# A two-layer hybrid decoder trunk: the adds that empty PSUM banks get a higher scheduling priority

## The chip, the cores and the metric

The kernel runs on one core of one Trainium2 chip. The metric is the device time of one execution in microseconds (us), and less is better. The median of three runs of the kernel before is 2667.34 us (2663.45 to 2671.42). The five engines of the core appear under their short names: PE is TensorE's matmul, PEld its weight load, DVE is VectorE, ACT is ScalarE, POOL is GpSimd and SP is SyncE, which issues nearly all loads.

## What is computed

The input is one sequence of 256 tokens of width 2048, in fp32. Two layers follow one another, each with a mixer and a feed-forward network (FFN); a final RMSNorm ends them.

```
for layer in (0, 1):
    x = x + mixer[layer](rms_norm(x, g_mix[layer]))      # 0: mLSTM heads and Mamba-2 heads; 1: attention
    x = x + swiglu(rms_norm(x, g_ffn[layer]), w_gate, w_up, w_down)
out = rms_norm(x, g_final)

def swiglu(x, w_gate, w_up, w_down):                     # w_gate, w_up: 2048 x 5632, w_down: 5632 x 2048
    return (silu(x @ w_gate) * (x @ w_up)) @ w_down
```

Only the two FFNs matter here. All weights come from HBM once.

## The kernel before

**Matmuls in three passes.** Each fp32 operand is split into a high part (rounded to the matmul's fp32r type) and a low part (what the rounding left). A product is three matmuls into the same bank: high times high, high times low, low times high (L383, L384, L385). The high part of a weight tile, `wh`, is a ScalarE copy (L355); its low part, `wl`, is a VectorE subtraction (L357).

**A step.** The FFN works in steps of 256 rows of the contraction dimension and 2 x 512 columns (for gate and up: 512 of each; for down: 1024 columns next to one another) by 256 tokens. A plain step (P) is four output tiles of 128 x 512 with two row blocks each, 8 products, 24 matmuls. A seven-product step (S) does the same 2 x 2 block product with seven products, 21 matmuls, in the manner of Strassen and Winograd. For that VectorE forms four sums of weight quarters (L364, L365, L367), so that an S step needs two weight tiles, the raw one and the sums, each with high and low parts. Below, "step 1, raw" and "step 1, sums" are these two.

**Strips and blocks.** `block` (L371) runs the steps of one strip. For gate and up the plan is P S P S P S P P, numbered 0 to 7; 11 strips cover the 5632 hidden columns, in groups of 4, 4 and 3. After each group `down` multiplies its hidden columns with w_down, in two blocks q of 1024 columns each (plan P S P S P P P P, or P S P S P P for the group of 3).

**PSUM.** There are eight banks of 128 x 512. Banks 0 to 3, `acc_f`, hold the four output tiles F of a block from its first to its last step. Banks 4 to 7, `acc_e`, hold the products E that S steps share between tiles. After the last S step (step 5 of a strip) the E banks are joined in four SBUF tiles `pre`: one ScalarE copy and four VectorE adds (L414 to L418). The two plain steps left go on into the F banks. At the end of a gate and up strip, `hidden` adds each F bank to its `pre` (L839), takes tanh on ScalarE (L842) and finishes the hidden values h on VectorE (L843, L844); then eight transposes on TensorE (L223) go into banks of the E ring, are split by L165 and L166, and make the operand of `down`. At the end of a down block, `add_all` adds `pre` and then F into the residual `xres` (L855): the pre part is called from inside `block` right after the last S step, the F part after the block has ended (L862). The next block's step 0 needs the four F banks again.

**Buffers.** A raw weight tile is loaded by two SP loads of 512 KB (L348). There are four buffers for raw tiles and sums, and three each for `wh` and `wl`, used in turn, so that the parts of a tile can be formed only when TensorE is done with the tile three places earlier.

**What sets the order.** All loops are unrolled and a list scheduler writes the order of each engine's instructions at build time: of those that it finds ready, it takes the one with the lowest priority number, which is the place in the program. A block under `tc.high_priority(offset=n)` is given numbers n lower. On the chip each engine runs its instructions in the order so written, with waits between engines. Weight work (`weights`, L340, its sums, copies and subtractions) stands under

```
        with tc.high_priority(offset=800):
            if not summed:
                return parts(raw, (slice(0, 2), slice(2, 4)))
```

while L414 to L418, L839 and L855 have no offset, and neither have L842 to L844 and the transposes.

Of the kernel before, what the change touches and what calls it, by code (L numbers as in the profile page):

```python
# [59 lines left out]
def hybrid_trunk(ctx: ExitStack, tc: tile.TileContext, a: dict, out: bass.AP):  # L60
    nc = tc.nc
# [38 lines left out]
    def blk(shape, name, dt=F32):  # L100
        return held_tile("blk", shape, name, dt)
# [7 lines left out]
    def t2(shape, name, dt=F32):  # L109
        return tmp.tile(shape, dt, tag="tmp", name=name)  # L110
# [7 lines left out]
    def bank(i, name):  # L118
        return psm.tile([P, 512], F32, tag=f"b{i}", name=name)
# [67 lines left out]
    def tick():  # L187
        clock[0] += 1
        run_until(lambda p: held[0] or p[0] > clock[0])
# [6 lines left out]
    class KT:  # L196
# [5 lines left out]
        def block(self, b):  # L202
            if self.blocks[b] is None:
                self.blocks[b] = self.home([P, 4, 2, T], f"{self.name}{b}", F32R)
            return self.blocks[b]
# [54 lines left out]
    def transpose_later(kt, b, src, gcol, wait, step=1):  # L260
        for half in range(2):
            later(wait + half * step, (kt.name, b), transpose_split, kt, b, src, gcol, half)
# [107 lines left out]
    def block(src, kt, row, nk, plan, after_sums=None, lead=1):  # L370

        n = nk // 2
        plan = plan[:n]
        F = [None] * 4
        pre = None
        E = {}

        def add(dst, a, b, start, stop):
            (ah, al), (bh, bl) = a, b
            nc.tensor.matmul(dst, ah, bh, start=start, stop=False)  # L383
            nc.tensor.matmul(dst, ah, bl, start=False, stop=False)  # L384
            nc.tensor.matmul(dst, al, bh, start=False, stop=stop)  # L385

        first_s, last_s = plan.find("S"), plan.rfind("S")
        turn["aux"] = 0
        group = []
        for j in range(n):  # L390
            if plan[j] == "S":
                held[0] = True
                wh, wl, sh, sl = weights(src, row + 2 * j * P, True)
                tok = lambda k, t: tuple(x[:, t * P:(t + 1) * P] for x in kt.parts(k))
                k2, k1 = 2 * j, 2 * j + 1
                a11, a12, a22 = tok(k1, 0), tok(k2, 0), tok(k2, 1)
                sk = kt.sums[j]
                s1, s2, s3, s4 = [(sk[:, i, 0, :], sk[:, i, 1, :]) for i in range(4)]
                b21, b11, b22 = [(wh[:, i, :], wl[:, i, :]) for i in range(3)]
                t3, t1, t2_, t4 = [(sh[:, i, :], sl[:, i, :]) for i in range(4)]  # L400
                prod = {1: (a11, b11), 2: (a12, b21), 3: (s4, b22), 4: (a22, t4),
                        5: (s1, t1), 6: (s2, t2_), 7: (s3, t3)}
                for p in (2, 3, 1, 7, 5, 6, 4):
                    if p in (2, 3, 4):
                        i = p - 2
                        add(F[i], *prod[p], start=False, stop=False)
                    else:
                        if p not in E:
                            E[p] = bank({1: 4, 7: 5, 5: 6, 6: 7}[p], "acc_e")
                        add(E[p], *prod[p], start=j == first_s, stop=j == last_s)  # L410
                if j == last_s:
                    pre = [t2([P, STRIP], "pre") for _ in range(4)]
                    p1, v, u3, w = pre
                    nc.scalar.copy(p1, E[1])  # L414
                    nc.vector.tensor_add(v, p1, E[6])
                    nc.vector.tensor_add(u3, v, E[7])
                    nc.vector.tensor_add(v, v, E[5])
                    nc.vector.tensor_add(w, u3, E[5])  # L418
                    if after_sums is not None:
                        after_sums(pre)  # L420
            else:
                group.append((j, weights(src, row + 2 * j * P, False)))
                if len(group) < lead and j < n - 1 and n - j <= lead:
                    continue
                for i in range(4):
                    t, s = divmod(i, 2)
                    first = F[i] is None
                    if first:
                        F[i] = bank(i, "acc_f")
                    for jj, (wh, wl) in group:  # L430
                        for kk in range(2):
                            xh, xl = kt.parts(2 * jj + kk)
                            ts = slice(t * P, (t + 1) * P)
                            add(F[i], (xh[:, ts], xl[:, ts]), (wh[:, 2 * s + kk, :], wl[:, 2 * s + kk, :]),
                                start=first and jj == group[0][0] and kk == 0, stop=jj == n - 1 and kk == 1)
                group = []
            tick()
            if j == last_s:
                held[0] = False
        return F, pre  # L440
# [168 lines left out]
    v = [blk([P, MH, MDV + 8], f"v{t}")[:, :, :MDV + 1] for t in range(NT)]  # L609
# [215 lines left out]
    def ffn(xt, r, wg_, wu_, wd, name, finish, begin=None):  # L825

        rh = cst.tile([P, NT], F32, tag="rh", name="rh" + name)
        rr = cst.tile([P, NT], F32, tag="rr", name="rr" + name)
        nc.vector.tensor_scalar(rh, r, 0.5, None, op0=OP.mult)
        nc.vector.tensor_mul(rr, rh, r)  # L830

        def hidden(hT, i, s, plan):
            F, pre = block(((wg_, s * STRIP), (wu_, s * STRIP)), xt, 0, KD, plan)
            hs = []
            for t in range(NT):
                g, u = F[2 * t], F[2 * t + 1]
                if pre is not None:
                    for p, f in zip(pre[2 * t:2 * t + 2], (g, u)):
                        nc.vector.tensor_add(p, p, f)  # L839
                    g, u = pre[2 * t:2 * t + 2]  # L840
                h = t2([P, STRIP], "h")
                nc.scalar.activation(h, g, AF.Tanh, scale=rh[:, t:t + 1])  # L842
                nc.vector.scalar_tensor_tensor(h, h, 1.0, g, op0=OP.add, op1=OP.mult)  # L843
                nc.vector.scalar_tensor_tensor(h, u, rr[:, t:t + 1], h, op0=OP.mult, op1=OP.mult)  # L844
                hs.append(h)
            transpose_later(hT, i, hs, None, 1, 0)

        def down(hT, first, n, last):
            for q in range(2):
                c0 = 2 * q * STRIP  # L850
                dst = [xr_[t][:, c0 + n_ * STRIP:c0 + (n_ + 1) * STRIP] for t in range(NT) for n_ in range(2)]

                def add_all(what):
                    for d, x in zip(dst, what):
                        nc.vector.tensor_add(d, d, x)  # L855

                if last and begin is not None:
                    begin(2 * q)
                    begin(2 * q + 1)
                F, _ = block(((wd, c0), (wd, c0 + STRIP)), hT, first * STRIP, 4 * n, PLAN_H[n], add_all,  # L860
                             lead=2 if last and q and name == "b" else 1)
                add_all(F)  # L862
                if last:
                    for s in (2 * q, 2 * q + 1):
                        finish(s)

        ring["aux"] = (6, 7, 4, 5)
        first = 0
        for n in (4, 4, 3):
            hT = KT(f"h{name}{first}", 4 * n)  # L870
            hT.sums = {j: None for j in range(2 * n) if PLAN_H[n][j] == "S"}
            for i in range(n):
                hidden(hT, i, first + i, PLAN_X)
            down(hT, first, n, first + n == DFF // STRIP)
            first += n
        ring["aux"] = (6, 7)
        turn["acc"] = 4
# [155 lines left out]
```

## Time and profile before

| | |
|---|---|
| median of 3 runs | 2667.34 us |
| profiled execution, its time | 2665.1 us |
| its span, first to last instruction | 2663.0 us |
| mean granted TensorE clock | 0.994 |
| PE busy | 2596.1 us (97%) |
| PEld busy | 2146.9 us (81%) |
| DVE busy | 2036.7 us (76%) |
| ACT busy | 1416.9 us (53%) |
| read from HBM | 492.39 MB, 186 GB/s over the span |

The profile is one execution, recorded by the hardware profiler. In the span, 0 to 780 us are the mixer of layer 0 and its output projection, 780 to 1530 the first FFN, 1530 to 1930 the attention layer, 1930 to the end the second FFN and the last norm. Rows of grouped instructions read: line, engine, operation, written tile <- read tiles, shape, count, then busy time and mean duration in ns, then the engine's idle time just before them and what ended it. Rows of waits read: engine, tile and line that waited <- what it waited for: total us, number of times, longest. Rows of stretches read: from:to, length, busy us (and instructions) of PE, PEld, DVE, ACT and POOL, granted clock, busy share of the DMA engines, GB/s. Rows of a timeline read: start, duration, instruction, how many are merged, and in brackets the idle time before it with what ended it. Matmuls are pipelined: a 128 x 512 matmul has a duration of about 0.39 us in the profile, and one starts every 0.227 us.

### The profile page before, as it was taken

What the parts mean: (1) busy time and instruction counts of PE and PEld (TensorE: products, weight loads), DVE (VectorE), ACT (ScalarE), POOL (GpSimd) and SP (SyncE); (2) the same over time, 40 slices, a digit from 0 to 9 for tenths busy, and PEclk for the clock granted to TensorE, in tenths of its full rate; (3) what the DMA queues carried; (4) which work ended last, traced back from release to release, by engine and by line L of the source; (5) the groups of instructions that cost most, each with busy time, mean ns of one, the idle gap of its engine ahead of it and who ended that gap; (6) DMA issues with size and microseconds to landing.
All of it is one profiled execution on the core that took longest, in us unless ns stands there. A gap on an engine that the chain in (4) does not pass through costs nothing.

```text
span 2663.0 us, 32578 instructions
## 1 busy us (share of the span) xinstructions
PE 2596.1 (97%) x12255; PEld 2146.9 (81%) x12255; DVE 2036.7 (76%) x2568; ACT 1416.9 (53%) x1886; POOL 46.8 (2%) x97
## 2 busy tenths in 40 slices
PE   8999999999999999999999999999999999999997
PEld 7888888888887778778887788888877787778876
DVE  5675777755558988898789766666698878987897
ACT  5455665665445554555454555556554545454554
POOL 2000010000000000000000000000000000000000
PEclk9999999999999999999999999999999999999999
DMA  7566676566645555656565465556465655565654
GB/s 231 167 191 182 184 228 190 166 189 216 189 156 189 191 198 188 203 186 203 176 206 173 143 191 173 173 173 205 142 215 175 206 175 204 175 206 175 207 171 150
DMA packets 254765, 496.66 MB, mean 187 GB/s; under 512 B 15704, under 2 KB 16096, under 8 KB 254352
## 3 DMA queue, kind: packets, MB, share of 16 engines
q1 hardware_dynamic: 250816, 484.57, 56.5%
q0 software_dynamic: 2896, 8.51, 1.2%
q8 instruction: 96, 1.57, 0.2%
q10 hardware_dynamic: 896, 1.52, 0.2%
q14 instruction: 61, 0.50, 0.1%
HBM read 492.39 MB, written 2.14 MB: 186 GB/s over the span
## 4 chain that ended last, share of the span: by engine, by line
PE 71%; DVE 16%; DMA 7%; issue 4%; ACT 2%; SPq 0%; POOL 0%; DVEq 0%; ACTq 0%; POOLq 0%
PE acc_w L304 11%; DVE wl L357 9%; PE acc_f L383 8%; PE acc_f L384 8%; PE acc_f L385 8%; PE acc_a L334 8%; PE acc_a L336 8%; PE acc_a L335 8%; PE acc_w L306 5%; DMA raw<-in_l_ffn_up 4%; DMA raw<-in_l_ffn_down 2%; ACT wh L355 2%; DVE sums L364 1%; PE p_tr L223 1%; PE acc_e L383 1%
## 5 line engine op out<-in xcount | busy, mean ns | idle before, releaser
L290 DVE TENSOR_TENSOR wl<-raw,wh 128x1024 fp32r<-128x1024 f32 (+1 forms) x385 | 469.8, 1221 | 324.7 <-ACT wh L289 323.1
L355 ACT CAST wh<-raw 128x1024 fp32r<-128x1024 f32 (+1 forms) x438 | 477.9, 1139 | 373.6 <-PE acc_f L385 295.3
L357 DVE TENSOR_TENSOR wl<-raw,wh 128x1024 fp32r<-128x1024 f32 (+1 forms) x438 | 563.6, 1329 | 119.7 <-ACT wh L355 119.7
L289 ACT CAST wh<-raw 128x1024 fp32r<-128x1024 f32 (+1 forms) x385 | 403.1, 1047 | 391.1 <-PE acc_a L336 181.4
L383 PE MATMUL acc_f<-wh,x 128*128 128x512 f32 x1012 | 397.2, 394 | 25.0 <-DVE pre L839 23.9
L384 PE MATMUL acc_f<-wl,x 128*128 128x512 f32 x1012 | 397.9, 393 | 1.3 <-DVE wl L357 1.2
L385 PE MATMUL acc_f<-wh,x 128*128 128x512 f32 x1012 | 395.9, 391 | 0.0
L355 ACT CAST wh<-sums 128x1024 fp32r<-128x1024 f32 x180 | 182.2, 1051 | 227.5 <-PE acc_f L385 89.1
L304 PE MATMUL acc_w<-xa,wh 128*128 128x512 f32 x768 | 275.9, 403 | 1.1 <-DVE xa L169 1.1
L383 PEld LDWEIGHTS acc_f<-wh,x 128*128 128x128 f32 x1012 | 190.9, 189 | 72.6 <-DVE pre L839 31.1
L357 DVE TENSOR_TENSOR wl<-sums,wh 128x1024 fp32r<-128x1024 f32 x180 | 213.4, 1220 | 23.1 <-ACT wh L355 23.1
L384 PEld LDWEIGHTS acc_f<-wl,x 128*128 128x128 f32 x1012 | 191.2, 189 | 47.8 <-DVE wl L357 8.4
L385 PEld LDWEIGHTS acc_f<-wh,x 128*128 128x128 f32 x1012 | 191.1, 189 | 39.5
L306 PE MATMUL acc_w<-xa,wl 128*128 128x256 f32 x768 | 215.5, 282 | 0.0
L304 PE MATMUL acc_w<-x,wh 128*128 128x512 f32 x512 | 185.0, 405 | 0.0
L304 PEld LDWEIGHTS acc_w<-xa,wh 128*128 128x128 f32 x768 | 144.9, 189 | 34.2 <-ACT wh L289 1.5
L334 PE MATMUL acc_a<-wh,xa 128*128 128x512 f32 x384 | 151.4, 394 | 0.0
L336 PE MATMUL acc_a<-wh,xa 128*128 128x512 f32 x384 | 151.2, 394 | 0.0
L335 PE MATMUL acc_a<-wl,xa 128*128 128x512 f32 x384 | 150.2, 391 | 0.0
L306 PEld LDWEIGHTS acc_w<-xa,wl 128*128 128x128 f32 x768 | 145.6, 190 | 0.8
L306 PE MATMUL acc_w<-x,wl 128*128 128x256 f32 x512 | 143.4, 281 | 0.0
L364 DVE TENSOR_TENSOR sums<-raw 128x1024 f32<-128x1024 f32 x90 | 109.9, 1221 | 27.2 <-DMA raw<-in_l_ffn_up 20.7
(320 smaller groups left out, 4612.2 us busy)
## 6 DMA issues: line engine op xcount, KB each, us to landing
raw<-in_l_w_in SPq DMA_DIRECT2D x191, 512.0 KB, 3.6
raw<-in_l_ffn_gate SPq DMA_DIRECT2D x176, 512.0 KB, 3.9
raw<-in_l_ffn_up SPq DMA_DIRECT2D x176, 512.0 KB, 4.8
raw<-in_l_ffn_down SPq DMA_DIRECT2D x176, 512.0 KB, 5.2
raw<-in_l_w_qkv SPq DMA_DIRECT2D x96, 512.0 KB, 3.6
raw<-in_l_w_out SPq DMA_DIRECT2D x64, 512.0 KB, 4.6
raw<-in_l_w_o SPq DMA_DIRECT2D x32, 512.0 KB, 4.7
rows<-scr POOLq DMA_DIRECT2D x10, 512.0 KB, 6.1
```

Of the source, the lines that this page charges most:

```text
L289: nc.scalar.copy(wh[:, ks, :], raw[:, ks, :])
L290: nc.vector.tensor_sub(wl[:, ks, :], raw[:, ks, :], wh[:, ks, :].bitcast(F32))
L304: nc.tensor.matmul(banks[f], wh[:, kk, fs], kt.both(k), start=k == 0, stop=False, skip_group_check=True)
L306: nc.tensor.matmul(banks[f][:, :T], wl[:, kk, fs], kt.parts(k)[0], start=False, stop=k == nk - 1, skip_group_check=True)
L334: nc.tensor.matmul(banks[t], xh[:, ts], wh[:, kk, :], start=k == 0, stop=False)
L335: nc.tensor.matmul(banks[t], xh[:, ts], wl[:, kk, :], start=False, stop=False)
L336: nc.tensor.matmul(banks[t], xl[:, ts], wh[:, kk, :], start=False, stop=k == nk - 1)
L355: nc.scalar.copy(h[:, c, :], of[:, c, :])
L357: nc.vector.tensor_sub(l[:, c, :], of[:, c, :], h[:, c, :].bitcast(F32))
L383: nc.tensor.matmul(dst, ah, bh, start=start, stop=False)
L384: nc.tensor.matmul(dst, ah, bl, start=False, stop=False)
L385: nc.tensor.matmul(dst, al, bh, start=False, stop=stop)
```

## The change

Three places get `tc.high_priority(offset=1600)`: the join of the E banks, the four adds of the F banks at the end of a gate and up strip, and the last call of `add_all`, which adds the F banks of a down block into the residual. Their offset is then larger than the 800 of the weight work. The additions of `pre` to the residual inside a down block, the tanh, L843, L844 and the transposes keep their place. No instruction is added or taken away.

```diff
@@ block, after the last S step
                     p1, v, u3, w = pre
-                    nc.scalar.copy(p1, E[1])
-                    nc.vector.tensor_add(v, p1, E[6])
-                    nc.vector.tensor_add(u3, v, E[7])
-                    nc.vector.tensor_add(v, v, E[5])
-                    nc.vector.tensor_add(w, u3, E[5])
+                    with tc.high_priority(offset=1600):
+                        nc.scalar.copy(p1, E[1])
+                        nc.vector.tensor_add(v, p1, E[6])
+                        nc.vector.tensor_add(u3, v, E[7])
+                        nc.vector.tensor_add(v, v, E[5])
+                        nc.vector.tensor_add(w, u3, E[5])
                     if after_sums is not None:
                         after_sums(pre)
@@ hidden
                     for p, f in zip(pre[2 * t:2 * t + 2], (g, u)):
-                        nc.vector.tensor_add(p, p, f)
+                        with tc.high_priority(offset=1600):
+                            nc.vector.tensor_add(p, p, f)
@@ down
-                add_all(F)
+                with tc.high_priority(offset=1600):
+                    add_all(F)
```

## The prediction

> **What bounds the kernel now.** I read the page first, then busy time by stage, then what TensorE waited for, then one strip boundary in the timeline of TensorE and VectorE.
>
> ```profile
> span 2663.0 us, 32578 instructions
> PE 2596.1 (97%) x12255; PEld 2146.9 (81%) x12255; DVE 2036.7 (76%) x2568; ACT 1416.9 (53%) x1886; POOL 46.8 (2%) x97
> ```
>
> ```profile
> 780.00:1530.00 750.00, 725.96 (x3194) 587.80 (x3192) 644.43 (x727) 383.97 (x420) 1.38 (x2) 0.99 0.55 185
> 1930.00:2663.00 733.00, 700.00 (x3069) 566.55 (x3068) 631.43 (x710) 369.10 (x396) 1.10 (x2) 0.99 0.56 187
> 888.34:932.75 44.41, 43.02 (x192) 34.91 (x192) 40.71 (x48) 24.38 (x26) 0.00 (x0) 1.00 0.57 190
> ```
>
> TensorE (first busy column) bounds the span. The two FFN stages (780 to 1530 and 1930 to 2663) hold 24.0 + 33.0 = 57 us of its 66.9 us of idle time; only they contain the changed lines, so the change can give at most about that, plus what a slow clock costs. One strip of 512 gate and up columns (third row) takes 44.4 us, TensorE busy 43.0, VectorE (third busy column) 40.7: VectorE is close behind.
>
> ```profile
> PE acc_f L383 <- DVE pre L839: 29.5, 21, 1.9
> PE acc_f L383 <- DVE xres L855: 5.1, 4, 2.4
> PE acc_e L384 <- DVE wl L357: 4.1, 6, 1.5
> ```
>
> Half of TensorE's idle time is one wait: the first matmul into an F bank, for the add (L839) that empties the bank of the strip before, 21 times, 1.4 us each. Low parts of weights (wl) cost it only 4.1 us. One boundary, TensorE first, then VectorE:
>
> ```profile
> 927.80 0.39 PE L383 MATMUL acc_f<-wh,x 128*128 128x512 f32 x1
> 930.97 0.39 PE L385 MATMUL acc_e<-wh,skx 128*128 128x512 f32 x1
> 932.75 0.50 PE L383 MATMUL acc_f<-wh,x 128*128 128x512 f32 x1 [1.39 <-DVE pre L839]
> 936.97 1.03 PE L223 MATMUL p_tr<-ident,h 128*128 128x128 f32 x8
> 937.76 0.48 PE L383 MATMUL acc_f<-wh,skx 128*128 128x512 f32 x1
> ```
>
> ```profile
> 913.49 4.63 DVE L357 TENSOR_TENSOR wl<-raw,wh 128x1024 fp32r<-128x1024 f32 x4 [1.22 <-ACT wh L355]
> 918.13 1.23 DVE L364 TENSOR_TENSOR sums<-raw 128x1024 f32<-128x1024 f32 x1
> ...
> 923.34 0.68 DVE L416 TENSOR_TENSOR pre<-pre,acc_e 128x512 f32<-128x512 f32 x1
> 923.94 0.68 DVE L839 TENSOR_TENSOR pre<-pre,acc_f 128x512 f32<-128x512 f32 x1
> 924.54 1.75 DVE L357 TENSOR_TENSOR wl<-raw,wh 128x1536 fp32r<-128x1536 f32 x1
> 926.21 0.68 DVE L417 TENSOR_TENSOR pre<-pre,acc_e 128x512 f32<-128x512 f32 x1
> 926.80 1.21 DVE L364 TENSOR_TENSOR sums<-raw 128x1024 f32<-128x1024 f32 x1
> 927.94 0.68 DVE L418 TENSOR_TENSOR pre<-pre,acc_e 128x512 f32<-128x512 f32 x1
> 928.54 0.68 DVE L365 TENSOR_TENSOR sums<-raw,sums 128x512 f32<-128x512 f32 x1
> 929.14 2.35 DVE L357 TENSOR_TENSOR wl<-sums,wh 128x1024 fp32r<-128x1024 f32 x2
> 931.41 0.68 DVE L367 TENSOR_TENSOR sums<-raw,sums 128x512 f32<-128x512 f32 x1
> 932.01 0.68 DVE L839 TENSOR_TENSOR pre<-pre,acc_f 128x512 f32<-128x512 f32 x1
> ...
> 934.47 0.68 DVE L839 TENSOR_TENSOR pre<-pre,acc_f 128x512 f32<-128x512 f32 x1
> ...
> 935.79 0.75 DVE L844 SCALAR_TENSOR_TENSOR h<-pre,rra,h 128x512 f32<-128x512 f32 x1
> ```
>
> The next strip's first matmul starts at 927.80. Between the first L839 (923.94) and the second (932.01) VectorE does 8 us of the next strip's weights; TensorE has 15 matmuls that need no other bank, then stands until 932.75.
>
> A stall also costs afterwards. The last column but two is the granted clock:
>
> ```profile
> 840.00:845.00 5.00, 5.00 (x13) 3.92 (x14) 4.75 (x8) 1.22 (x2) 0.00 (x0) 0.54 0.54 201
> 1493.00:1497.00 4.00, 3.72 (x10) 2.96 (x11) 2.02 (x4) 2.67 (x8) 0.00 (x0) 0.56 0.28 105
> 1966.00:1971.00 5.00, 4.82 (x15) 3.79 (x16) 3.95 (x8) 1.67 (x2) 0.00 (x0) 0.66 0.53 196
> 2233.00:2238.00 5.00, 4.88 (x14) 3.90 (x15) 3.88 (x7) 0.73 (x1) 0.00 (x0) 0.66 0.60 207
> ```
>
> ```profile
> 837.46 0.59 PE L384 MATMUL acc_e<-wl,skx 128*128 128x512 f32 x1 [1.52 <-DVE wl L357]
> 839.79 0.79 PE L383 MATMUL acc_f<-wh,x 128*128 128x512 f32 x1 [1.32 <-DVE pre L839]
> ```
>
> Two stalls within 2.4 us are followed by five microseconds at 0.54: 5 x 0.46 = 2.3 us lost. The other three stretches lose 4 x 0.44 = 1.8, 5 x 0.34 = 1.7 and 1.7; they follow the longest boundary stalls. 7.5 us in all, 1.8 of it (1493) behind the wait for xres.
>
> The Trainium skill, "TensorE: Matmul & The Clock Gate", section "What's actually happening", says that the clock halves only after an idle window of about 3.4 us. By that rule none of these stalls, each under 2.5 us, would slow the clock, and the clock term below would be nothing; the measured 0.54 decides against it.
>
> **The change part by part.** No instruction is added or removed; three groups are put ahead of weight work in VectorE's order (and the ACT copy L414 in ScalarE's). The order in which the two built programs' instructions stand shows it: until the end of the first strip both are the same; after that the adds of the E banks (L415 to L418) stand between the low parts of the strip's last two weight tiles, and the four L839 between the next strip's first sums, instead of behind the weights for its steps 1 and 3. TensorE's order follows: 24 matmuls of the next strip's step 0 in a row, in place of 6, 9 of step 1, 18.
>
> (1) *F banks.* I walk VectorE through the new order from 913.49. Pitches from the rows above: a 128x1024 low part 4.64 / 4 = 1.16, a 128x512 add 0.60 (923.34 to 923.94), a 128x1536 part 1.67, the large sum 1.14. Up to the first L839 stand six low parts, one 128x512 part of activations, four E adds and one sum: 7.0 + 0.6 + 2.4 + 1.1 = 11.1, so it starts at 924.6 and the second ends at 925.9. TensorE wants the second bank at 927.80 + 6 matmuls x 0.227 = 929.2. The third and fourth add, behind a small sum and the 128x1536 part, end at 928.8 and 929.4; wanted at 930.5 and 931.9. All four are early by 1.7 us or more, so the whole wait goes: 29.5 us. The bounds are 0 (all of it moves, below) and 29.5.
>
> (2) *Clock.* Without these stalls the three slow stretches behind them go: 2.3 + 1.7 + 1.7 = 5.7 us. Bounds 0 and 7.5.
>
> (3) *xres (L855, raised in its last call only).* An F add writes the slice that the unraised add of pre writes before it, and must follow it. In the new order these four still stand up to 14 instructions apart in the last column half. I count no gain: 0 of 5.1 + 1.8 us.
>
> (4) *What is late instead.* The work passed over: the last low parts of step 1, then the multiplies that finish h (L843, L844), then h's transposes. Continued at the same pitches: small sum 929.9, two low parts with one L843 between them 932.9, the sum for step 3 934.0, first L844 934.7, step 2's two low parts 937.0, step 3's sum, part and sum 939.9, L843 and L844 941.2. Before, the last L844 ended at 936.5 and all eight transposes went at 936.97. TensorE, unstalled: step 0 to 933.2, 15 matmuls of step 1 and two transposes to 936.8, 20 matmuls of step 2 to 941.3. There it needs the second h: just there. Low parts of step 2 (935.8, 937.0) are wanted at 936.8 and 938.4. Then come the transposes' banks, which are the E banks:
>
> ```profile
> L165 ACT CAST ha<-p_tr x5: 573/587/592, 896.1 to 986.4; 128x512 fp32r<-128x512 f32 x5
> L166 DVE TENSOR_TENSOR ha<-p_tr,ha x5: 680/684/692, 897.9 to 987.1; 128x512 fp32r<-128x512 f32 x5
> L364 DVE TENSOR_TENSOR sums<-raw 128x1024 f32<-128x1024 f32 x90 | 109.9, 1221 | 27.2 <-DMA raw<-in_l_ffn_up 20.7 <-DMA raw<-in_l_ffn_down 4.2 <-PE acc_a L336 0.7
> L855 DVE TENSOR_TENSOR xres<-xres,acc_f 128x512 f32<-128x512 f32 x48 | 32.2, 682 | 18.4 <-PE acc_f L385 18.4
> ```
>
> The six transposes end near 941.9, two ScalarE copies (0.59 each) at 943.2, while TensorE has four matmuls until 942.8: it waits 0.4 us; the VectorE part that frees the other bank can stand behind a sum waiting for its load (L364: 20.7 us there in the whole run). Each step used later passes this on, since there are only three buffers for high and low parts. I take 0.7 us a boundary, 22 boundaries (11 strips in each of two layers): 15 us. Bounds: 0, where TensorE finds other matmuls, and 1.5 + 2.3 = 3.8 a boundary, the 837.46 event with its slow clock; 0.7 is nearer to 0, because the walk gives 0.4 and low parts cost TensorE 4.1 us in all now.
>
> SP's queue: loads keep their order but for three places, where two loads of one weight tile change places with two of the next. The trace's loads take about 5 us and are wanted over 10 us later: nothing, unless VectorE frees the buffers late, which is part of (4).
>
> The Trainium skill, "PSUM — Partial Sum Buffer", section "Engine vs sequencer instructions", calls VectorE's queue strictly first in, first out: a raised add that is not ready holds the weights behind it. The trace agrees, L855 kept VectorE idle for 18.4 us in 48 adds. By my walk the raised adds are 0.6 us or more behind their banks, so this adds nothing; at 0.4 us for each of 88 adds VectorE would lose 34 us, and that case is inside the third rival.
>
> Sum: 29.5 + 5.7 + 0 - 15 = 20.2 us. The profiled execution took 2665.1 us with 2663.0 of span; 2665.1 - 20 = 2645. The runs' median, 2667.3, is 2.2 higher; I forecast 2646.
>
> **The rivals.** (a) *All of it is gained.* TensorE's order has other matmuls at each place in (4), and the xres waits shrink too: 29.5 + 7.5 + 5.1 = 42, 2625. For it: in the clean half of the strips the order takes nothing apart. Against: VectorE's 40.7 of 44.4 us leaves little to catch up with. (b) *The wait only moves*, to E banks or low parts, one for one: 35.2 / 22 = 1.6 us a boundary, 2667. (c) *Slower: low parts come late.* Place: the second half of step 3's weights, whose buffers come free only when the E matmuls held up by the late transposes are done. In 12 strips of the new order these matmuls stand taken apart and mixed with step 4's; in 2 of the old one, and one of these two led to the 837.46 event. At 3.8 us in the 16 strips that follow a strip: 61 - 35 = 26, 2693; in the ten new ones alone, 38 + 5 for the rest - 35 = 8, 2675. It decides from 1.6 us a boundary. For it, the missing cover in (4); against, that event needed VectorE to be behind at a boundary as well, which the raised adds prevent for the banks. (d) *No slow clock to regain* (the skill's rule above): without the 5.7 the sum is 14.5, 2651 to 2653; the rows speak against it, chance 0.05, counted within the forecast.
>
> **How the numbers follow.** Forecast (2634 to 2659) 0.46, (a) 0.20, (b) 0.13, (c) 0.21. A difference under 0.3% (8 us) is about what a measurement of this kernel can't tell from none, so (b) is "same". Faster is 0.66, same 0.13, slower 0.21. The range goes from 2622 (under which some 0.08 of (a) lies) to 2684 (some 0.1 of (c) above).
>
> **What would show it.** TensorE's wait for L839 under 5 us; wait for ACT's p_tr copies, wl or wh of some 10 to 20 us in its place; no granted clock under 0.7 within the FFN strips; strip period near 43.5 us; ScalarE's wait of h on L839 mostly gone. The forecast is wrong if TensorE's waits for wl pass 30 us, if 0.5 clocks come more often, or if L839 itself waits for TensorE for more than a few us.

## The result and the profile after

The changed kernel takes 2609.12 us (median of four runs, 2607.17 to 2611.76); beside it the kernel before took 2669.38 us. The ratio is 0.9778 [0.9757, 0.9798]: 60 us faster, where 20 were forecast, and below the range given. The profiled execution took 2609.47 us, that of before 2665.1, so the two traces are 55.6 us apart. From the page of the profile after, the span and the engines:

```profile
span 2607.7 us, 32610 instructions
PE 2579.4 (99%) x12255; PEld 2142.8 (82%) x12255; DVE 2039.9 (78%) x2568; ACT 1417.5 (54%) x1886; POOL 46.9 (2%) x97
```

The two FFN stages of the kernel after, as stretches:

```profile
780.00:1505.00 725.00, 718.74 (x3206) 587.22 (x3205) 648.09 (x729) 385.70 (x423) 1.38 (x2) 1.00 0.57 192
1880.00:2602.00 722.00, 715.79 (x3180) 584.64 (x3178) 647.72 (x728) 380.43 (x410) 1.80 (x3) 1.00 0.57 189
```

TensorE's waits of the kernel after, the largest that belong to the FFNs:

```profile
PE acc_f L383 <- DVE xres L857: 1.7, 1, 1.7
PE acc_f L383 <- ACT wh L355: 1.1, 2, 0.9
...
PE acc_e L383 <- ACT wh L355: 1.0, 2, 0.5
PE acc_f L384 <- DVE wl L357: 1.0, 2, 0.6
```

The wait for the adds that empty the F banks (L839 before, L841 here) is gone from the list, and nothing of size has taken its place: TensorE has 6.3 + 6.2 = 12.5 us of idle time in the two stages, where it had 57.0. From the first FFN matmul's start to the last one's, the stages take 709.1 and 705.3 us where they took 736.1 and 735.0; the time between them is the same (391.1 before, 391.8 after). So all of the gain, 27.0 + 29.7 = 56.7 us, lies in the FFNs.

To see where it came from I put down, for every two TensorE instructions that follow one another in the FFN stages of the timeline, the distance of their starts beyond the usual 0.227 us for a matmul and 0.098 us for a transpose. It belongs to the releaser that the later one, or a weight load between them, shows; the distance right after a stall, some 0.11 us longer than usual, is counted with the stall, and any other matmul pitch of 0.33 to 0.48 us without a releaser is put down as slow clock. The same was done for each experiment below (us, both FFNs together). The last column is from the order of TensorE's instructions as built: in how many of the 34 strips and down blocks the 24 matmuls of step 0 stand in a row.

| kernel | FFN stages | F adds | high and low parts (wh, wl) | xres | late h, ha, hb, xg | slow clock | step 0 whole |
|---|---|---|---|---|---|---|---|
| before | 1471.1 | 36.0 | 20.6 | 6.9 | 0.5 | 5.7 | 5 |
| after | 1414.4 | 0 | 7.0 | 1.9 | 5.3 | 0 | 32 |
| F adds alone | 1442.0 | 13.5 | 13.9 | 7.4 | 3.5 | 3.2 | 10 |
| join (E adds) alone | 1479.9 | 6.8 | 58.6 | 2.1 | 5.9 | 8.6 | 3 |
| last down add alone | 1459.6 | 35.9 | 18.1 | 2.0 | 0.8 | 2.4 | 12 |
| F and down | 1434.3 | 13.6 | 13.4 | 1.9 | 3.6 | 1.8 | 17 |
| join and down | 1472.4 | 6.5 | 53.8 | 0.6 | 6.2 | 7.3 | 10 |
| h alone | 1498.0 | 49.0 | 19.9 | 7.2 | 0.6 | 20.2 | 5 |
| after, rank 800 | 1416.4 | 0 | 7.6 | 2.2 | 4.8 | 1.3 | 32 |
| after, h raised | 1408.3 | 0 | 7.6 | 2.0 | 0.4 | 0 | 32 |
| after, h and xres raised | 1404.8 | 0 | 6.3 | 0 | 0.4 | 0 | 34 |
| before, weights unranked | 1405.1 | 0 | 6.6 | 0.8 | 0 | 0 | 33 |

From before to after: F adds 36.0, clock 5.7, xres 5.0, and 13.6 from fewer waits for the parts of weights, which no term of the prediction had; against it stand 4.8 of new waits for what is now late. That is 55.5 of the 56.7 us, and small unnamed gaps are the rest.

The boundary that the prediction walked through, in the kernel after: VectorE's timeline first, then rows of TensorE's matmuls and weight loads.

```profile
914.24 0.68 DVE L419 TENSOR_TENSOR pre<-pre,acc_e 128x512 f32<-128x512 f32 x1
914.84 1.22 DVE L357 TENSOR_TENSOR wl<-raw,wh 128x1024 fp32r<-128x1024 f32 x1
915.98 1.22 DVE L364 TENSOR_TENSOR sums<-raw 128x1024 f32<-128x1024 f32 x1
917.11 1.28 DVE L841 TENSOR_TENSOR pre<-pre,acc_f 128x512 f32<-128x512 f32 x2
918.31 0.68 DVE L365 TENSOR_TENSOR sums<-raw,sums 128x512 f32<-128x512 f32 x1
918.91 1.75 DVE L357 TENSOR_TENSOR wl<-raw,wh 128x1536 fp32r<-128x1536 f32 x1
920.58 1.27 DVE L841 TENSOR_TENSOR pre<-pre,acc_f 128x512 f32<-128x512 f32 x2
...
931.64 0.75 DVE L846 SCALAR_TENSOR_TENSOR h<-pre,rra,h 128x512 f32<-128x512 f32 x1
932.30 0.68 DVE L845 SCALAR_TENSOR_TENSOR h<-h,pre 128x512 f32<-128x512 f32 x1
933.02 0.75 DVE L846 SCALAR_TENSOR_TENSOR h<-pre,rra,h 128x512 f32<-128x512 f32 x1
```

```profile
932.44 0.44 PE L223 MATMUL p_tr<-ident,h 128*128 128x128 f32 x2
933.87 0.83 PE L223 MATMUL p_tr<-ident,h 128*128 128x128 f32 x6
```

```profile
933.83 0.64 PEld L223 LDWEIGHTS p_tr<-ident,h 128*128 128x128 f32 x6 [0.22 <-DVE h L846]
936.47 0.19 PEld L383 LDWEIGHTS acc_e<-wh,skx 128*128 128x128 f32 x1 [0.37 <-DVE ha L166]
```

The four F adds stand within 4.7 us (917.11 to 921.85), where they took 11.2 (923.94 to 935.15, the prediction's rows). The price stands in the rows behind: h is ready 16.7 us after the first add, the transposes go in two portions at the end, and TensorE waits 0.2 to 0.4 us for h and ha.

### The profile page after: what moved, and what is told of

Its sections match the earlier page's. It is cut to its first block, busy times and chain, and to the rows that moved or that the text cites. A ratio compares the mean times of both kernels' runs of the same rounds, so it can differ in the third digit from the quotient of the medians.

```text
span 2607.7 us, 32610 instructions
## 1 busy us (share of the span) xinstructions
PE 2579.4 (99%) x12255; PEld 2142.8 (82%) x12255; DVE 2039.9 (78%) x2568; ACT 1417.5 (54%) x1886; POOL 46.9 (2%) x97
## 4 chain that ended last, share of the span: by engine, by line
PE 94%; DVE 3%; DMA 1%; issue 1%; ACT 1%; SPq 0%; POOL 0%; ACTq 0%; POOLq 0%; DVEq 0%
PE acc_f L384 14%; PE acc_f L385 14%; PE acc_f L383 14%; PE acc_w L304 11%; PE acc_a L334 8%; PE acc_a L336 8%; PE acc_a L335 8%; PE acc_w L306 6%; PE acc_e L383 3%; PE acc_e L384 3%; PE acc_e L385 3%; PE p_tr L223 2%; DVE wl L357 1%; PE p_y L763 1%; DMA raw<-in_l_ffn_up 0%
```

## The experiments

Two ideas were tried against one another first. **A**: the three raised groups work independently, each on its own wait. **B**: they are one chain. An F add writes the tile that the join writes before it, so a raised add is held by a join that was not raised.

**F adds alone.**

```diff
                     for p, f in zip(pre[2 * t:2 * t + 2], (g, u)):
-                        nc.vector.tensor_add(p, p, f)
+                        with tc.high_priority(offset=1600):
+                            nc.vector.tensor_add(p, p, f)
```

> Only the four adds of the F banks in hidden (L839) get the offset of 1600; the join of the E banks and the last add_all of a down block keep their place. Theory A (the F adds alone were late, each part works by itself): nearly all of the 60 us comes back, 40 to 52 us faster than before, some 2620; TensorE's wait for L839 is under 4 us. Theory B (an F add writes the tile that the join writes first, so a join left behind the weights holds the raised adds): 15 to 35 us faster, some 2645, and waits for L839 stay at 10 to 20 us.

Measured: 2637.62 us (2636.55 to 2639.8), ratio 0.9879 [0.9864, 0.9894], 33 us faster. The waits of TensorE in this kernel:

```profile
PE acc_f L383 <- DVE pre L840: 9.7, 13, 1.5
PE acc_f L383 <- DVE xres L856: 6.2, 3, 2.9
```

Over half of the gain comes from this one line, but a third of the F bank wait is still there, though the adds have the rank that they have in the changed kernel. Idea B had 15 to 35 us, and 10 to 20 us of this wait.

**The join alone.**

```diff
-                    nc.scalar.copy(p1, E[1])
-                    nc.vector.tensor_add(v, p1, E[6])
...
+                    with tc.high_priority(offset=1600):
+                        nc.scalar.copy(p1, E[1])
+                        nc.vector.tensor_add(v, p1, E[6])
...
```

> Only the join of the E banks is raised. Theory A: no gain (within 5 us of before), since the next strip needs the E banks late and the L839 adds stay behind the weights. Theory B: also little by itself, 0 to 10 us faster, from F adds that can follow the join sooner; TensorE's wait for L839 stays above 20 us in both. Were it above 25 us faster, it is the join and not the F adds that held the boundary.

Measured: 2673.91 us (2670.08 to 2677.52), ratio 1.0016 [1.0007, 1.0026]: no gain, if anything 4 us lost. Its waits of TensorE:

```profile
PE acc_e L383 <- ACT wh L355: 14.2, 21, 0.9
PE acc_e L384 <- DVE wl L357: 12.4, 11, 1.6
PE acc_f L383 <- ACT wh L355: 8.2, 26, 0.9
...
PE acc_f L383 <- DVE pre L840: 1.2, 4, 0.5
```

Here the wait did only move. The F bank wait falls by 29 us in the table, and the waits for parts of weights rise by 38. Both ideas had missed this: they left the wait for the F adds above 20 us, and its row reads 1.2. The built order shows with what it goes together: in 22 of the 34 blocks step 0 is taken apart behind its twelfth matmul, with parts of step 1 and of step 2 or 3 between its pieces, so that the weight tiles of several steps are in use at once; there are three buffers for parts.

**The last down add alone.**

```diff
-                add_all(F)
+                with tc.high_priority(offset=1600):
+                    add_all(F)
```

> Only the last add_all of a down block is raised. Both theories: the waits for xres shrink from 6.9 us to 2 to 5 us by the spacing of the matmuls, the waits for L839 stay at 30 us or more, 2 to 7 us faster than before.

Measured: 2660.46 us (2653.22 to 2661.51), ratio 0.996 [0.9946, 0.9973], 10 us faster, more than the 2 to 7 expected. TensorE's wait at the strips stays as it was:

```profile
PE acc_f L383 <- DVE pre L839: 29.9, 21, 1.9
```

The xres waits fall from 6.9 to 2.0 us, and over half of the slow clock goes with them (5.7 to 2.4).

**F adds and the last down add**, both edits from above.

> F adds and the last add_all of a down block raised, the join not. Theory A: 50 to 60 us faster, the whole change but for some 5 us. Theory B: 20 to 40 us faster; the join is worth 20 us or more on top of the F adds though it is worth little alone.

Measured: 2628.34 us (2624.83 to 2629.64), ratio 0.9841 [0.9826, 0.9856], 42 us faster, about the 33 + 10 of the two alone: these add up. TensorE's wait for the F adds is that of the F adds alone:

```profile
PE acc_f L383 <- DVE pre L840: 9.6, 15, 1.5
```

What the changed kernel has beyond this one is the raised join: 0.9841 - 0.9778 = 0.0063 of 2670 us, 17 us (each of the two ratios is known to 0.002 or better, some 5 us). Alone it was worth nothing. In the table the waits for the F adds go from 13.6 to 0 with it and those for parts from 13.4 to 7.0. That speaks for B, though B had put this kernel at 20 to 40 us and the join at 20 or more.

**The join and the last down add**, the missing combination.

> The changed kernel without its raised F adds: the join of the E banks and the last add of the down projections are raised. Together with the five kernels of before, F, E and down alone, F with down, and all three, it fills the table of parts. Theory B (the join is worth its 18 us only because the raised F adds stand behind it): without raised F adds the join adds nothing to the down part, 2655 to 2666 us. Theory A (the parts add up: the join is worth 18 us beside the down part): 2640 to 2648 us.

Measured: 2666.06 us (2662.04 to 2671.27), ratio 0.9976 [0.9966, 0.9987], at the upper end of what B expected (2666) and far from A. Its waits of TensorE are much like those of the join alone:

```profile
PE acc_e L383 <- ACT wh L355: 12.5, 17, 0.9
PE acc_e L384 <- DVE wl L357: 10.7, 9, 1.3
```

So the join is worth +4 us alone (0.0016 of 2670), +4 us beside the down add (0.9976 - 0.996), and -17 us beside the F adds. B is supported, A is out.

**The raised groups at the rank of the weights**: 800 in place of 1600 at all three places of the changed kernel.

> The changed kernel with the three raised groups at the rank of the weight work (800) and not above it (1600). Theory B (what counts is that no weight work of a later step stands ahead of the adds): at equal rank the program's order decides, and the adds come before the weights of the next strip in it; the built order of TensorE is that of the changed kernel. So 2609 us, within 5 either way, TensorE's waits for the F adds under 2 us. Rival (the adds must stand ahead of weights already listed before them too): waits for the F adds of 5 us or more come back, with the time at 2615 to 2630.

Measured: 2610.29 us (2606.73 to 2612.36), ratio 0.9773 [0.9755, 0.979], the same as the changed kernel. At 800 and at 1600 the result is the same: once the adds aren't ranked below the weights, the program's order puts them in front of the next strip's.

**h raised too**, on top of the changed kernel.

```diff
-                nc.scalar.activation(h, g, AF.Tanh, scale=rh[:, t:t + 1])
-                nc.vector.scalar_tensor_tensor(h, h, 1.0, g, op0=OP.add, op1=OP.mult)
-                nc.vector.scalar_tensor_tensor(h, u, rr[:, t:t + 1], h, op0=OP.mult, op1=OP.mult)
+                with tc.high_priority(offset=1600):
+                    nc.scalar.activation(h, g, AF.Tanh, scale=rh[:, t:t + 1])
+                    nc.vector.scalar_tensor_tensor(h, h, 1.0, g, op0=OP.add, op1=OP.mult)
+                    nc.vector.scalar_tensor_tensor(h, u, rr[:, t:t + 1], h, op0=OP.mult, op1=OP.mult)
```

> The changed kernel with the three instructions that make h from the adds' results (a ScalarE tanh, two VectorE multiplies, for both token tiles) raised as well. They are what the prediction's step (4) called late: in the changed kernel TensorE now waits for h, ha, hb and xg some 5 us in the FFN stages, and its order takes the transposes of h apart. Theory (late h is what is left of the debt): the eight transposes stand together right after step 0, those waits fall under 1.5 us, the FFN stages get 3 to 6 us shorter, 2603 to 2607 us. Rival (VectorE has no room: what goes to h early is taken from low parts): 4 x 0.75 = 3 us of VectorE work stand ahead of step 1's low parts in each of 22 strips; TensorE's waits for wl and wh in F and E matmuls rise from 7 us to 15 or more, and the time is 2612 to 2625 us.

Measured: 2602.55 us (2600.91 to 2606.33), ratio 0.9747 [0.973, 0.9764], 8 us below the kernel with rank 800 on the same chip. The transposes go in one portion again, some 8 us earlier than in the kernel after, and the waits for late h and its parts fall from 5.3 to 0.4 us, while those for parts of weights stay (7.0, 7.6). TensorE's timeline at the same boundary:

```profile
924.01 1.03 PE L223 MATMUL p_tr<-ident,h 128*128 128x128 f32 x8
938.41 0.50 PE L384 MATMUL acc_e<-wl,skx 128*128 128x512 f32 x1 [0.85 <-DVE wl L357]
```

The debt that the prediction feared exists, and it is late h: 5 us in the table, 8 us of run time, which one more raised block pays back.

**h and the join's adds to xres raised too.**

```diff
                     if after_sums is not None:
-                        after_sums(pre)
+                        with tc.high_priority(offset=1600):
+                            after_sums(pre)
```

> As the kernel before in this list, and the adds of the join's results to xres in the down projections (four after the join of each block) are raised too, so that the whole chain join, xres, F adds stands in the order in which it must run. Theory (the chain holds what follows it, in the down blocks as in the gate and up blocks): the xres waits of 1.9 us in the FFN stages fall under 1 us, 0.5 to 3 us better than with h alone. Rival (12 such places are too few, and each puts four adds of 0.6 us ahead of the next strip's weights): no difference beyond 2 us, or 2 to 4 us worse.

Measured: 2599.04 us (2596.86 to 2601.38), ratio 0.9732 [0.9715, 0.9749], 3.5 us better than with h alone, a little more than was expected; the intervals overlap. The xres waits of the FFN stages are gone.

**Weights without a rank**, the kernel before with one number changed.

```diff
-        with tc.high_priority(offset=800):
+        with tc.high_priority(offset=0):
             if not summed:
                 return parts(raw, (slice(0, 2), slice(2, 4)))
```

> The kernel before, with the raised rank of the weight work (high parts, low parts, sums) taken away, and nothing else raised: adds, h and weights then stand by the program's order everywhere. Theory (all of the gain is the rank of the adds against that of the weights): the boundaries come out as in the changed kernel or better, 2600 to 2612 us, no wait for the F adds above 2 us. Rival (the weights' rank is needed: with none, VectorE does adds, h and the norm's work first, and the low parts come late in the FFN stages and in the stages between): TensorE's waits for wl and wh rise to 20 us or more, 2620 to 2660 us.

Measured: 2598.82 us (2597.51 to 2601.87), ratio 0.9732 [0.9712, 0.9752]. It is the opposite route, nothing raised, and it arrives where the long list of raised blocks does. So the kernel before lost its time to the rank of its weight work, which let the next strip's weights overtake everything that closes the strip before. Both of these kernels beat the changed one by 11 us (beside the kernel with rank 800, which ran on the same chip: 2610.29 against 2599.04 and 2598.82). TensorE's largest waits in the FFNs are now

```profile
PE acc_e L383 <- ACT wh L355: 1.9, 3, 0.8
...
PE acc_f L383 <- ACT wh L355: 0.5, 1, 0.5
```

**h alone**, the three instructions of h raised in the kernel before, the adds in front of them not.

> The kernel before with only the three instructions raised that make h out of the F adds' results; the F adds in front of them stay where they were. Theory B (a raised instruction is held by an unraised one that it needs): nothing moves, 2664 to 2674 us, and TensorE's wait for the F adds stays at 25 to 33 us. Rival (early transposes alone are worth the 6 us that they gave on top of the changed kernel): 2658 to 2664 us.

Measured: 2691.39 us (2689.81 to 2692.91), ratio 1.0073 [1.0058, 1.0088]: 20 us slower, which neither idea had; the two profiled executions are 28 us apart (spans 2691.0 and 2663.0). Its waits of TensorE, its VectorE timeline at the same boundary, and two of its stretches:

```profile
PE acc_f L383 <- DVE pre L839: 41.7, 21, 3.0
```

```profile
931.21 1.23 DVE L357 TENSOR_TENSOR wl<-sums,wh 128x1024 fp32r<-128x1024 f32 x1
932.34 0.69 DVE L844 SCALAR_TENSOR_TENSOR h<-h,pre 128x512 f32<-128x512 f32 x1
932.95 1.23 DVE L357 TENSOR_TENSOR wl<-sums,wh 128x1024 fp32r<-128x1024 f32 x1
934.08 0.69 DVE L367 TENSOR_TENSOR sums<-raw,sums 128x512 f32<-128x512 f32 x1
934.68 1.29 DVE L839 TENSOR_TENSOR pre<-pre,acc_f 128x512 f32<-128x512 f32 x2
```

```profile
1155.00:1160.00 5.00, 5.00 (x15) 3.99 (x16) 3.15 (x5) 0.72 (x1) 0.00 (x0) 0.66 0.57 205
2295.00:2300.00 5.00, 4.49 (x13) 3.55 (x14) 3.67 (x6) 0.72 (x1) 0.00 (x0) 0.66 0.63 210
```

The first multiply of h needs only the first F add, so it isn't held as B had it, and B holds only for what needs the result of an unraised instruction. It goes ahead of the second F add (932.34 against 934.68), which therefore comes one multiply later: 0.6 us at each of 21 boundaries is 12.6, and the row has grown by 41.7 - 29.5 = 12.2. The rest is the clock: slow matmuls cost 20.2 us in place of 5.7. A raise of something that isn't on the path, past something that is, was paid for twice here, in the wait and in the clock.

**More work on VectorE**, in the kernel with unranked weights: adds of 128x128 behind each strip's h, results unused.

```diff
+            if pre is not None:
+                with tc.high_priority(offset=0):
+                    for _ in range(8):
+                        nc.vector.tensor_add(junk, pre[0][:, 0:128], pre[2][:, 0:128])
             transpose_later(hT, i, hs, None, 1, 0)
```

> The kernel with unranked weights, and eight VectorE adds of 128x128 more after each strip's h, whose results nobody uses: about 8 x 0.28 us (an add of that size in the trace before) = 2.3 us of VectorE a strip, 11 strips in each FFN stage, 25 us a stage. In the kernel without them VectorE is busy 632 us of 700 in the FFN stage, so 68 us are left. Theory (that idle time is cover, the boundaries pay only for order): under 5 us longer, 2599 to 2604 us. Rival (as step (4) of the prediction has it, VectorE is so close behind that what is late is passed on): a third of the 50 us or more comes through, 2615 us and up, with waits for wl over 15 us.

> As the kernel before in this list with sixteen adds a strip, about 4.6 us, 50 us a stage of the 68 left. Theory (cover): up to 20 us longer, since the adds come in one stretch right behind the boundary, 2600 to 2620 us. Rival (passed on): 2640 us and up, slower than half of the gain.

Measured: 2615.25 us (2614.07 to 2616.18), ratio 0.9788 [0.9773, 0.9802], with eight adds, and 2632.55 us (2631.02 to 2634.71), ratio 0.9853 [0.9836, 0.9869], with sixteen. Each add took 0.287 us, about the 0.28 expected, but they stand scattered among the weight work and overlap their neighbours in the trace, so that one lengthened VectorE's busy time by 0.18 only. Busy time of the engines in the kernel with unranked weights, then with eight and with sixteen adds:

```profile
PE 2571.3 (99%) x12255; PEld 2147.6 (83%) x12255; DVE 2039.6 (79%) x2568; ACT 1423.9 (55%) x1886; POOL 47.7 (2%) x97
```

```profile
PE 2580.2 (99%) x12255; PEld 2145.5 (82%) x12255; DVE 2070.9 (79%) x2744; ACT 1415.2 (54%) x1886; POOL 47.7 (2%) x97
```

```profile
PE 2587.1 (98%) x12255; PEld 2143.7 (81%) x12255; DVE 2105.7 (80%) x2920; ACT 1415.4 (54%) x1886; POOL 47.8 (2%) x97
```

VectorE got 31.3 and 66.1 us more work, and the time grew by 16.4 and 33.7 (by the ratios, since the kernel with unranked weights ran on another chip, 15 and 32): about half of it comes through, at either dose, as waits for parts of weights (6.6, 18.6 and 38.4 us in the tabulation). Of sixteen adds, the waits of TensorE:

```profile
PE acc_e L383 <- ACT wh L355: 9.1, 16, 2.2
PE acc_f L384 <- DVE wl L357: 8.9, 15, 2.4
```

The idea that VectorE's idle 10% is cover has fallen. With eight adds the time is where the rival began (2615 and up); with sixteen it lies between the two (up to 2620, and 2640 and up), since only half is passed on. One reservation: TensorE's built order also changed with the added work (seven-product steps taken apart in 18 of 22 strips, against 2 without it), and the two effects aren't separated.

## Why the prediction was wrong

The direction was right and so was the first mechanism, the F banks; the size was not, 20 us forecast and 57 in the profile. Of the 35 us between the sum of 20.2 and the 55.5 that the table names, 23.8 lie in step (4), 6.5 in (1) and 5.0 in (3). (A slip beside it: the runs' median less the sum is 2647, not 2646.) Step by step:

- **(1) F banks, 29.5 us: right, and undersized.** All of it went, as the walk had it; the tabulation gives 36.0. The wait's row counts idle time after the end of the matmul before. At the 932.75 boundary it says 1.39, while the starts, 930.97 and 932.75, are 1.78 apart, 1.55 more than the pitch, and the next start comes another 0.11 late. The Trainium skill, "Perfetto Trace Analysis", section "Tensor Engine Instruction (MATMUL, LD_WEIGHTS)", says that the end of such an instruction is an estimate made from its size; the trace fits that, with matmuls of 0.39 us that start every 0.227. A price for a stall of TensorE has to come from starts.
- **(2) Clock, 5.7 us: right, the exact figure by luck.** The term took three of the four slow stretches, by the granted clock; the 5.7 of the table are all four, by the starts of matmuls. No matmul pitch of the slow kind is left in the FFN stages of the kernel after. Rival (d), by the rule of an idle window of about 3.4 us (the Trainium skill, "TensorE: Matmul & The Clock Gate", section "What's actually happening"), has no room: the kernel with h alone lost 20.2 us to slow matmuls, and no stall of its FFN stages is longer than the 3.0 us at the end of its row.
- **(3) xres, 0 us: wrong.** 5.0 us were gained, and the last down add alone made the kernel 10 us faster, with the clock that recovers. I had seen that these adds must follow the adds of pre and took that for a hold; but of the four waits in the row before (5.1 us), raising the last add alone left one (1.2 us).
- **(4) The debt, 15 us lost: the step that failed; it was a gain of 8.8.** Its walk was good: it had the last transpose of h end 17.3 us after the first F add began (924.6 to 941.9), and the trace has 17.6 (917.11 to 934.70); it had a wait of 0.4 us for the transposes' banks and the row says 0.37. But I took 0.7 us a boundary, because "each step used later passes this on". It didn't: the new waits are 4.8 us in all, 0.2 a boundary. And the waits for parts of weights, to which the lateness should have been passed, fell from 20.6 to 7.0 us, a gain of 13.6 that no rival had, not even (a), which came out 16 us short. There was no room for it in the sum: I had read that low parts cost TensorE 4.1 us "in all", but that row is the low parts for the E banks alone. With the other rows for parts (1.2, 2.2 and 1.6) the idle time is 9.1 us, and from start to start the table has 20.6.

Why did they fall? Among the kernels without added work, TensorE's order goes with it. With step 0 whole in 32 to 34 blocks these waits are 6 to 8 us, with 10 to 17 blocks 13 to 18, with 5 blocks about 20, and 54 to 59 where the join is raised without the F adds. The link is the buffers for parts, and the trace shows it. In the kernel before, I count 45 waits of TensorE for parts, weight loads included, 18.5 us together (without the first three tiles, whose buffers were empty). In 43 of them ScalarE's copy of the awaited tile had started within 0.1 us of the end of TensorE's last matmul on the tile that lay at the same address before it: the copy could not have been earlier. With the join alone that holds for 80 of 86. One case, the last matmul of a strip's step 7, the copy into its buffer, and the matmul that waits for the copy:

```profile
833.87 0.39 PE L385 MATMUL acc_f<-wh,x 128*128 128x512 f32 x1
834.34 2.00 ACT L355 CAST wh<-sums 128x1024 fp32r<-128x1024 f32 x2 [4.00 <-PE acc_f L385]
835.44 0.50 PE L383 MATMUL acc_e<-wh,skx 128*128 128x512 f32 x1 [0.50 <-ACT wh L355]
```

Of the 18.5 us, 10.8 are for tiles of step 1, into buffers that the last steps of the block before had held: the order takes matmuls of step 1 forward, in front of the rest of step 0, and so wants their parts early. Another 5.5 are for step 2, whose buffer a broken step 0 held until its last matmul. In the kernel after these are 2.2 and 0.1. In the two kernels with added work step 0 is whole too (33 and 32 blocks), but only 11 of 50 and 14 of 71 copies follow so closely on the buffer: there something else is late. VectorE's waits before and after, a row of each:

```profile
DVE wl L357 <- ACT wh L355: 142.7, 79, 6.7
```

```profile
DVE wl L357 <- ACT wh L355: 81.2, 73, 3.1
```

That is 61.5 us of VectorE's idle time gone. I counted the weights as overtaken, and left out that they had been waiting for TensorE, which had been waiting for the adds. No run changed the number of buffers, so what more of them would give stays open.

The signs named: the wait for L839 under 5 us, yes (0); no slow clock in the strips, yes; 10 to 20 us of waits for p_tr copies or parts instead, no; a strip period near 43.5 us, no, this strip took 42.8 (877.32 to 920.12) where it had taken 44.4; the wait of ScalarE's h on the adds mostly gone, no, it was a little more than halved. Rows of ScalarE's waits, before and after:

```profile
ACT h L842 <- DVE pre L839: 76.4, 22, 4.8
```

```profile
ACT h L844 <- DVE pre L841: 31.4, 27, 2.2
```

Of the queue that a raised add might hold, the row of the adds says that VectorE stood 2.6 us in all before them:

```profile
L841 DVE TENSOR_TENSOR pre<-pre,acc_f 128x512 f32<-128x512 f32 x88 | 58.5, 683 | 2.6 <-PE acc_f L385 1.2
```

Rival (b), the wait only moves, is what the join does alone. Rival (c), parts come late by over 1.6 us a boundary, happened in none of the raised kernels with the F adds among them; the two kernels with added work show that late parts do cost time (12 and 32 us more of such waits), not that they come late where (c) had it. None of the prediction's three signs of being wrong showed up: all three looked for a slower kernel.

## What to carry to other kernels

Where a list scheduler has a rank for prefetched work, look at what that rank overtakes: here one number at the weights cost some 70 us, and taking it away did as much as raising the join, the adds and h. Raise the whole chain that frees a buffer, or take away the rank that overtakes it: single links were worth from 4 us lost to 33 gained, and the wrong one cost 20. And an order built around a stall holds buffers and wants others early, so a stall's price is not only its own length: ask who waits for the engine that waits.

## What the runs showed of the hardware

The granted clock falls after stalls far shorter than 3 us, and not by a fixed threshold. In the kernel before, stalls at L839 of 1.4 us (8) were never followed by a stretch at half clock (pitch over 0.4 us), of 1.6 us one in 8, and that one had another stall, of 1.04 us, 2.3 us before it. With h alone, of 2.0 to 2.15 us 4 in 9, of 2.2 us all 6; one of 2.96 us was not, nor was one of 2.20 us at the xres adds in the kernel before. The section of the Trainium skill named under (2) calls the window free-running. A stall that falls in one window or across two would give such a mixture, but no run varied that. By the starts of its matmuls a slow stretch cost 1.3 to 2.2 us in the kernel before, and about 1.6 with h alone (20.2 us in 13 stretches). So, as an estimate from these counts, cutting a stall of 2.2 us to 1.4 gains some 2 us rather than 0.8.

VectorE, with one tenth of its time idle in these stages, passed half of the work added in these two kernels on to the end, TensorE's changed order included. A share of busy time well under 100% was no cover here.
